# Order and spacing of the weight sums that a decoder step makes in DRAM

## The chip, the cores and the metric

One core of a Trainium2 chip runs the whole step as one program. The metric is the time of one execution in microseconds on the device. Three runs of the kernel before gave 1013.59, 1014.58 and 1017.05 us, median 1014.58. One more execution was taken with the hardware profiler: 1010.48 us, of which the span from the first to the last instruction is 1008.7 us.

Engines are named as in the profile: PE (TensorE, matmuls), PEld (its weight loads), DVE (VectorE), ACT (ScalarE), POOL (GpSimd), SP (SyncE, which issues most DMAs).

## The reference, cut to what matters

One layer of a hybrid decoder is applied to 512 prompt tokens and 8 x 4 sample tokens, 544 tokens in all, in float32:

```python
z = x @ w_in                                        # 1024 -> 6656: values and gates of two mixers
ca = silu(layer_norm(causal_dwconv(a_val * sigmoid(a_gate))))     # 31 taps
y_a = ca @ w_proj_a
hs = rg_lru(causal_dwconv(b_x))                     # 4 taps, two gate products, a scan
y_b = (hs * gelu(b_gate)) @ w_proj_b
mix = (sigmoid(g_a) * y_a + sigmoid(g_b) * y_b) @ w_out
x1 = layer_norm(ALPHA * x + mix)
ff = square(relu(x1 @ w_ff1)) @ w_ff2               # 1024 -> 4096 -> 1024
ple = sigmoid(x1 @ w_ple_gate) * (p @ w_ple_proj)
y = layer_norm(ALPHA * x1 + ff + ple)
```

The new convolution and scan states are outputs too. The change concerns w_ff1 and w_ff2 alone, and the time before they are used.

## The kernel before, in words

Activations lie with channels on the 128 partitions and the 544 tokens along the free dimension. Each float32 factor is split into a high part and the remainder (hi, lo), and a product is three matmuls: hi by hi, hi by lo, lo by hi. Weights are loaded by SP in chunks of 512 KB into `raw` (three buffers, line 38), ACT copies `hi`, DVE subtracts to get `lo`.

The step runs in the order of `ORDER` (line 52): input products of the two mixers (a, x, g, b, c), the gate products of the recurrence (r), then proj_b (p), the per-layer input (s) and proj_a (q), then w_out with the first layer norm, w_ple_gate, and last the MLP. While PE does the input products, DVE runs the 31-tap convolution (`ca`, line 734) as a chain of 30 multiply-adds for each of eight channel tiles. GpSimd makes the products of the sample tokens' taps (`prod`), the short convolution of the sample tokens (`cbs`, line 844), the running sum `sum_a`, the product of the input gate (`gg`), and after each scan the copy `hl` and the product `gate` (line 900).

The MLP uses a scheme of seven products in place of eight for blocks of two by two. A panel is one pair of output tiles; its weight has four blocks A11, A12, A21, A22. Of the seven products three use blocks as they are (A11, A22, A12) and four use sums of blocks:

- S3 = A11 + A21
- S1 = A21 + A22
- S2 = A22 + S3
- S4 = A12 + S2

No compute engine makes these sums. For each, SP copies one block from DRAM to a tile in DRAM (`sum...`), and then GpSimd issues a DMA that adds the other operand to that tile (line 246). S2 therefore needs a finished S3, and S4 a finished S2; S1 needs neither. There are 15 panels of w_ff1 (1 to 15, each sum 256 KB) and 4 of w_ff2, whose sums are made in two column parts c = 0 and 1 (each 384 KB): 60 + 32 = 92 sums, so 92 copies and 92 adds, 28.3 MB each.

The order of all instructions on all engines is written by a planner that runs when the program is built. `Clocks` (line 88) keeps a time for each engine and prices each operation; `Clocks.op` (line 125) lets a step start when its engine and its operands are ready by those clocks. An add is priced with 1.0 us of GpSimd and is ready some 3 us after its share of a common sum stream; a copy with 0.47 us of SP. `fill` (line 413) lets each engine take its next step as long as its clock is less than a given lead ahead of PE's. It asks `stream` (line 336) first, and `stream` asks `sum_stream` (line 261) first of all: with k = (PE's planner time - SUM_FROM) / SUM_EVERY, the n-th copy (from 0) may go when n < k + COPY_AHEAD, and the n-th add when n < k and its copy is out. So sums go out at an even pace, ahead of whatever else SP or GpSimd could do, and take their place on the two queues among the weight loads and among GpSimd's arithmetic. Each engine then works through its own list in order.

In the MLP, units (one block or sum of one panel) go through `fraw` on SP, `fhi` on ACT and `flo` on DVE (`add_unit`, line 1242); SP may be 7 units ahead of PE, ACT 5, DVE 4 (line 29). A unit that is a sum is loaded only once its add was issued (line 1280 issues it on the spot otherwise). The panels run in the order of line 34: w_ff1's panel 0 by plain products, then panels 1 to 3, then four passes over w_ff2 with further panels of w_ff1 after each: 4 to 6, 7 to 9, 10 to 13, and 14 and 15. Passes 0 and 1 over w_ff2 use part c = 0 of its sums, passes 2 and 3 part c = 1.

Of the kernel before, what the change touches and what calls it, by code (L numbers as in the profile page):

```python
# [9 lines left out]
F32 = mybir.dt.float32  # L10
F32R = mybir.dt.float32r
AF = mybir.ActivationFunctionType
OP = mybir.AluOpType
AX = mybir.AxisListType

P = 128
# [17 lines left out]
PANELS = [(1, p, None) for p in (1, 2, 3)]  # L34
for _g, _ps in enumerate(((4, 5, 6), (7, 8, 9), (10, 11, 12, 13), (14, 15))):
    PANELS += [(2, _p, _g) for _p in range(4)] + [(1, _p, None) for _p in _ps]
SUM_FROM, SUM_EVERY, COPY_AHEAD = 40.0, 6.0, 3
RAW_BUFS = 3
SPLIT_BUFS = 4
LOAD_AHEAD = 5  # L40
# [47 lines left out]
class Clocks:  # L88

    STEP = 0.13  # L90
    SETS = {AF.Sigmoid: 1, AF.Exp: 2, AF.Tanh: 2, AF.Sqrt: 3, AF.Gelu_apprx_tanh: 4}
# [68 lines left out]
def tile_hybrid_step(ctx: ExitStack, tc: tile.TileContext, I, O):  # L160
# [5 lines left out]
    dpool = ctx.enter_context(tc.tile_pool(name="sums", bufs=1, space=bass.MemoryType.DRAM))  # L166
# [22 lines left out]
    def cols(t, h):  # L189
# [4 lines left out]
    TE, V, S, G, DMA = (Engine(clocks, k, e) for k, e in  # L194
                        zip("TVSGD", (nc.tensor, nc.vector, nc.scalar, nc.gpsimd, nc.sync)))
# [37 lines left out]

    lead = [LEAD]
    sums, summed_up, to_copy, to_add = {}, set(), deque(), deque()
    for kind, n in [(1, p) for p in (1, 2, 3)] + [(2, p) for p in range(4)] + [(1, p) for p in range(4, 16)]:
        w = I["w_ff1" if kind == 1 else "w_ff2"][n]
        ncol = 512 if kind == 1 else 6 * P
        for c in range(kind):
            cs = slice(c * ncol, c * ncol + ncol)  # L240
            s = {nm: dpool.tile([P, ncol], F32, name=f"sum{kind}_{n}_{c}_{nm}") for nm in ("S3", "S1", "S2", "S4")}
            for nm, own, src in (("S3", w[0, :, cs], w[2, :, cs]), ("S1", w[2, :, cs], w[3, :, cs]),
                                 ("S2", w[3, :, cs], s["S3"]), ("S4", w[1, :, cs], s["S2"])):
                sums[kind, n, c, nm] = s[nm]
                to_copy.append(lambda to=s[nm], own=own: DMA.dma_start(to, own))
                to_add.append((lambda to=s[nm], src=src: G.dma_start(to, src, accum_op=OP.add, max_dma_last_dim=1024),
                               (kind, n, c, nm)))
    n_adds = len(to_add)

# [1058 lines left out]
    for n, k in in_turn():  # L1308
        kind, p, g = PANELS[n]
        if k == 1:  # L1310
            first_unit[kind, p if kind == 1 else g] = min(len(units), first_unit.get((kind, p if kind == 1 else g), INF))
        nm = FORM[k]
        q0, nq = (0, 4) if kind == 1 else GROUPS[g]
        key = (kind, p, 0 if kind == 1 else g // 2, nm)
        if nm in BLOCK:
            w, made = I["w_ff1" if kind == 1 else "w_ff2"][p, BLOCK[nm], :, q0 * P:(q0 + nq) * P], lambda: True
        else:
            c0 = 0 if kind == 1 else g % 2 * 3 * P
            w, made = sums[key][:, c0:c0 + nq * P], lambda key=key: key in summed_up
# [301 lines left out]
    for n, k in in_turn():  # L1621
        kind, p, g = PANELS[n]
# [96 lines left out]
```

## Time and profile before

| what | before |
|---|---|
| median of 3 runs | 1014.58 us |
| the profiled execution | 1010.48 us |
| its span | 1008.7 us |
| PE busy | 935.5 us |
| DVE busy | 793.7 us |
| ACT busy | 496.1 us |
| POOL busy | 254.2 us |
| first and last issue of a copy of the sums | 23.3 and 597.0 us |
| first and last issue of an add | 40.2 and 617.4 us |
| first and last load of a finished sum | 596.5 and 926.4 us |

Busy shares are means over stages with different bounds, so the table of stretches in the prediction is the better guide. In the rows of a timeline the columns are the start, the length, the engine and line, the operation with its output and inputs, the number of like instructions merged, and in brackets how long the engine had been idle before and what released it. Line 155 is the helper through which every instruction goes, so tiles and not lines tell the instructions apart. In the lists of waits, a row gives who waited for whom, the total in us, the number of times and the longest.

### The profile page before, as it was taken

Reading aid. Unit: us, or ns where it says so; the run is one execution under the profiler, and the core shown is the slowest. Engines: PE = TensorE matmul, PEld = TensorE weight load, DVE = VectorE, ACT = ScalarE, POOL = GpSimd, SP = SyncE. Lnnn points to the kernel's source line nnn. Section 1 sums busy time; section 2 is a strip of 40 time slices with the busy share of each in tenths; the row PEclk is TensorE's granted clock in tenths of the full one; section 3 lists DMA queues with packets and bytes.
Section 4 is the critical chain, followed back from the end, with each engine's and each line's share of the span. In section 5 each row is a group of like instructions: output and inputs, shape, how many; then the busy total and the mean of one; then the engine's idle time right before and its main releaser. Section 6 shows DMA issues by size and latency. Waiting matters only on the chain.

```text
span 1008.7 us, 18589 instructions
## 1 busy us (share of the span) xinstructions
PE 935.5 (93%) x7236; PEld 924.7 (92%) x7236; DVE 793.7 (79%) x1337; ACT 496.1 (49%) x875; POOL 254.2 (25%) x265
## 2 busy tenths in 40 slices
PE   8999798975989797999999999999999999999895
PEld 8999798975979797999999999989999899989895
DVE  5799999899997998793356883979688686777547
ACT  6422236623449622562233772775674655854601
POOL 0453755675637621210421211000000000000002
PEclk9999988997989899999999999999999999999998
DMA  8557689875889594967869784446546446446412
GB/s 298 147 152 185 180 200 262 196 175 138 183 214 202 136 212 130 229 160 196 260 155 253 173 225 54 149 133 188 174 138 204 148 146 218 147 144 204 133 48 84
DMA packets 125272, 175.81 MB, mean 174 GB/s; under 512 B 9920, under 2 KB 97344, under 8 KB 124224
## 3 DMA queue, kind: packets, MB, share of 16 engines
q1 hardware_dynamic: 96064, 146.31, 45.0%
q0 software_dynamic: 29120, 28.32, 20.3%
q8 instruction: 57, 0.93, 0.4%
q14 instruction: 31, 0.25, 0.1%
HBM read 167.57 MB, written 60.44 MB: 226 GB/s over the span
## 4 chain that ended last, share of the span: by engine, by line
PE 47%; DVE 29%; DMA 7%; ACT 7%; issue 5%; POOL 4%; SPq 0%; DVEq 0%; POOLq 0%; ACTq 0%
PE psq L155 13%; PE ps L155 13%; DVE ca L155 11%; PE f L155 8%; PE g L155 6%; DVE lo L155 4%; ACT fy L155 2%; ACT fhi L155 1%; DMA fraw<-sum_S 1%; DMA sum_S<-in_w_ff_dram 1%; DVE flo L155 1%; PE pps L155 1%; DVE th L155 1%; ACT fz L155 1%; DMA sum_S<-sum_S 1%
## 5 line engine op out<-in xcount | busy, mean ns | idle before, releaser
L155 DVE SCALAR_TENSOR_TENSOR ca<-u,par_a,ca 128x482 f32<-128x482 f32 (+29 forms) x240 | 176.3, 792 | 0.3
L155 ACT ACTIVATE hi<-raw 128x1024 fp32r<-128x1024 f32 (+3 forms) x109 | 99.9, 929 | 130.3 <-PE ps L155 52.6
L155 ACT ACTIVATE fhi<-fraw 128x512 fp32r<-128x512 f32 (+1 forms) x229 | 124.3, 571 | 60.5 <-DMA fraw<-sum_S 21.7
L155 DVE TENSOR_TENSOR flo<-fraw,fhi 128x512 fp32r<-128x512 f32 (+1 forms) x229 | 138.2, 620 | 17.7 <-ACT fhi L155 17.4
L155 DVE TENSOR_TENSOR lo<-raw,hi 128x1024 fp32r<-128x1024 f32 (+3 forms) x105 | 122.2, 1178 | 25.4 <-ACT hi L155 25.4
L155 POOL TENSOR_TENSOR y<-y,rows_g 128x512 f32<-128x512 f32 x2 | 3.1, 1550 | 379.1 <-ACT y L155 379.1
L155 POOL DMA_DIRECT2D sum_S<-sum_S x46 | 45.3, 985 | 171.5 <-DMA sum_S<-sum_S 91.2
L155 PE MATMUL f<-x1h,fhi 128*128 128x272 f32 x212 | 59.6, 294 | 5.1 <-DVE fz L155 3.5
L155 POOL DMA_DIRECT2D sum_S<-in_w_ff_dram x46 | 51.8, 1198 | 28.5 <-DMA sum_S<-in_w_ff_dram 27.1
L155 PE MATMUL f<-x1h,flo 128*128 128x272 f32 x212 | 58.6, 289 | 0.2 <-DVE flo L155 0.2
L155 PE MATMUL f<-x1l,fhi 128*128 128x272 f32 x212 | 58.4, 288 | 0.0
L155 PE MATMUL ps<-x0h,hi 128*128 128x288 f32 x104 | 23.9, 313 | 29.6 <-ACT gate L155 14.6
L155 PEld LDWEIGHTS ps<-x0h,hi 128*128 128x128 f32 x104 | 16.9, 200 | 31.5 <-ACT gate L155 15.5
L155 PEld LDWEIGHTS f<-x1h,fhi 128*128 128x128 f32 x212 | 39.0, 189 | 7.3 <-DVE fz L155 5.4
L155 DVE TENSOR_TENSOR acc<-acc,g 128x272 f32<-128x272 f32 x80 | 34.8, 434 | 12.9 <-PE g L155 12.1
L155 PEld LDWEIGHTS f<-x1h,flo 128*128 128x128 f32 x212 | 38.9, 188 | 0.5 <-DVE flo L155 0.5
L155 PEld LDWEIGHTS f<-x1l,fhi 128*128 128x128 f32 x212 | 39.0, 189 | 0.0
L155 PE MATMUL psq<-x1l,hi 128*128 128x288 f32 (+1 forms) x128 | 36.9, 288 | 0.0
L155 PE MATMUL psq<-x1h,lo 128*128 128x288 f32 (+1 forms) x128 | 36.8, 288 | 0.0
L155 PE MATMUL psq<-x1h,hi 128*128 128x288 f32 (+1 forms) x128 | 36.8, 288 | 0.0
L155 POOL TENSOR_TENSOR prod<-ctx_a,par_a 128x248 f32<-128x248 f32 x32 | 30.9, 1150 | 0.0
L155 ACT ACT_TABLE_LOAD x20 | 25.7, 1283 | 1.1 <-PEq L1709 0.7
(1994 smaller groups left out, 3385.9 us busy)
## 6 DMA issues: line engine op xcount, KB each, us to landing
raw<-in_w_in_dram SPq DMA_DIRECT2D x51, 512.0 KB, 5.0
fraw<-in_w_ff_dram SPq DMA_DIRECT2D x65, 256.0 KB, 3.5
sum_S<-in_w_ff_dram SPq DMA_DIRECT2D x60, 256.0 KB, 5.3
fraw<-sum_S SPq DMA_DIRECT2D x60, 256.0 KB, 3.3
sum_S<-in_w_ff_dram SPq DMA_DIRECT2D x32, 384.0 KB, 5.8
fraw<-sum_S SPq DMA_DIRECT2D x64, 192.0 KB, 2.9
fraw<-in_w_ff_dram SPq DMA_DIRECT2D x48, 192.0 KB, 3.1
sum_S<-in_w_ff_dram POOLq DMA_DIRECT2D x30, 256.0 KB, 5.4
```

Source lines behind the costliest of these rows:

```text
L155: return fn(out, *args, **kw)
```

## The change

The sums are made in another order, at another pace, and copies run further ahead.

- Order: before, panel by panel, and within a panel S3, S1, S2, S4 in a row. After, in seven sets of three or four panels, and within a set form by form: S3 of all its panels, then S1 of all, S2 of all, S4 of all. The sets are w_ff1 1 to 3; w_ff2 part c = 0; w_ff1 4 to 6; 7 to 9; w_ff2 part c = 1; w_ff1 10 to 12; 13 to 15. Before, both parts of w_ff2 came right after w_ff1's panels 1 to 3.
- Distance: S4 comes three or four issues after the S2 that it needs (one before), S2 six or eight after its S3 (two before).
- Pace: SUM_FROM from 40.0 to 25.0, SUM_EVERY from 6.0 to 7.2, COPY_AHEAD from 3 to 4.

The sums themselves, their number and their sizes stay.

```diff
-SUM_FROM, SUM_EVERY, COPY_AHEAD = 40.0, 6.0, 3
+SUM_FROM, SUM_EVERY, COPY_AHEAD = 25.0, 7.2, 4
...
-    for kind, n in [(1, p) for p in (1, 2, 3)] + [(2, p) for p in range(4)] + [(1, p) for p in range(4, 16)]:
-        w = I["w_ff1" if kind == 1 else "w_ff2"][n]
-        ncol = 512 if kind == 1 else 6 * P
-        for c in range(kind):
-            cs = slice(c * ncol, c * ncol + ncol)
-            s = {nm: dpool.tile([P, ncol], F32, name=f"sum{kind}_{n}_{c}_{nm}") for nm in ("S3", "S1", "S2", "S4")}
-            for nm, own, src in (("S3", w[0, :, cs], w[2, :, cs]), ("S1", w[2, :, cs], w[3, :, cs]),
-                                 ("S2", w[3, :, cs], s["S3"]), ("S4", w[1, :, cs], s["S2"])):
-                sums[kind, n, c, nm] = s[nm]
-                to_copy.append(lambda to=s[nm], own=own: DMA.dma_start(to, own))
-                to_add.append((lambda to=s[nm], src=src: G.dma_start(to, src, accum_op=OP.add, max_dma_last_dim=1024),
+    SETS = ([(1, p, 0) for p in (1, 2, 3)], [(2, p, 0) for p in range(4)], [(1, p, 0) for p in (4, 5, 6)],
+            [(1, p, 0) for p in (7, 8, 9)], [(2, p, 1) for p in range(4)], [(1, p, 0) for p in (10, 11, 12)],
+            [(1, p, 0) for p in (13, 14, 15)])
+    for ps_ in SETS:
+        for nm in ("S3", "S1", "S2", "S4"):
+            for kind, n, c in ps_:
+                w = I["w_ff1" if kind == 1 else "w_ff2"][n]
+                ncol = 512 if kind == 1 else 6 * P
+                cs = slice(c * ncol, c * ncol + ncol)
+                s = sums[kind, n, c, nm] = dpool.tile([P, ncol], F32, name=f"sum{kind}_{n}_{c}_{nm}")
+                own, src = {"S3": (0, w[2, :, cs]), "S1": (2, w[3, :, cs]), "S2": (3, sums.get((kind, n, c, "S3"))),
+                            "S4": (1, sums.get((kind, n, c, "S2")))}[nm]
+                to_copy.append(lambda to=s, own=w[own, :, cs]: DMA.dma_start(to, own))
+                to_add.append((lambda to=s, src=src: G.dma_start(to, src, accum_op=OP.add, max_dma_last_dim=1024),
                                (kind, n, c, nm)))
```

## The prediction

> **What bounds the kernel now.** I read the page's busy shares first, then the waits, the table of stretches, and last the timelines of GpSimd and VectorE where the change acts.
>
> ```profile
> PE 935.5 (93%) x7236; PEld 924.7 (92%) x7236; DVE 793.7 (79%) x1337; ACT 496.1 (49%) x875; POOL 254.2 (25%) x265
> q1 hardware_dynamic: 96064, 146.31, 45.0%
> q0 software_dynamic: 29120, 28.32, 20.3%
> ```
> TensorE is busy 93% of 1008.7 us. q0 is GpSimd's DMA queue, which carries nothing but the 92 adds. The stretches say more than the mean; their columns are the stretch, its length, busy us of PE, PEld, DVE, ACT and POOL, granted clock, DMA share, GB/s:
>
> ```profile
> 100.00:400.00 300.00, 256.87 (x1927) 253.97 (x1925) 282.12 (x369) 136.85 (x187) 166.85 (x161) 0.92 0.80 186
> 400.00:600.00 200.00, 199.11 (x1553) 198.24 (x1554) 134.55 (x234) 95.98 (x169) 43.38 (x45) 0.99 0.80 203
> 617.00:711.00 94.00, 90.01 (x707) 88.28 (x706) 76.01 (x159) 58.17 (x124) 0.88 (x1) 1.00 0.48 142
> 617.00:946.00 329.00, 314.61 (x2465) 309.48 (x2463) 249.50 (x516) 203.00 (x431) 0.88 (x1) 1.00 0.51 158
> ```
> Between 100 and 400 us VectorE is the bound: 17.9 of 300 us idle, while TensorE idles 43 and runs at a clock of 0.92. From 400 on TensorE is the bound: 0.9 us idle in 200, and 14.4 in the 329 of the MLP.
>
> The change is aimed at this:
>
> ```profile
> POOL sum_S L155 <- DMA sum_S<-in_w_ff_dram: 107.4, 22, 11.7
> POOL sum_S L155 <- DMA sum_S<-sum_S: 91.2, 16, 9.9
> ```
> GpSimd stands 198.6 us in 38 waits in front of an add, for the DMA that makes its source or its own tile. That is a fifth of the span, on an engine that is busy a quarter of it. So the question is not how long it waits but what stands behind it on its queue.
>
> **What the removed waits are worth.** Two waits of the same length, from the timelines of GpSimd and VectorE (start, length, instruction, idle before it and its releaser):
>
> ```profile
> 148.38 0.94 POOL L155 DMA_DIRECT2D sum_S<-sum_S  x1 [9.19 <-DMA sum_S<-sum_S]
> 151.24 0.64 POOL L155 COPY st_u<-u 128x30 f32<-128x30 f32 x1 [0.65 <-DVE u L155]
> ...
> 194.15 1.52 POOL L155 DMA_DIRECT2D sum_S<-sum_S  x1
> 204.91 0.94 POOL L155 DMA_DIRECT2D sum_S<-sum_S  x1 [9.24 <-DMA sum_S<-sum_S]
> 205.52 2.05 POOL L155 COPY hl<-th 128x9 f32<-128x9 f32 x1
> ```
> ```profile
> 203.10 1.28 DVE L155 TENSOR_TENSOR_SCAN th<-aa,gg 128x544 f32<-128x544 f32 x1
> ```
> After the first, the next arithmetic on GpSimd still waits 0.65 us for VectorE: the wait cost nothing. The second is the one place I found where it cost something: the scan ends at 204.38, the copy that needs it starts at 205.52, so 1.1 us are lost, and they go on through the gate product to a wait of VectorE (hb0l, below). Behind the other waits of over 4 us I find, in the same timeline, the next non-DMA instruction released later by VectorE or ScalarE. So of 198.6 us of waits 1.1 us reach the bound. The chain of waits seems to say more, since it names sum DMAs. But there a step is put down to a semaphore that fell by chance:
>
> ```profile
> 132.13 4.07 DMA sum_S<-in_w_ff_dram
> 136.20 0.36 POOL cb L155
> ```
> ```profile
> 134.76 0.63 POOL L155 TENSOR_TENSOR cbs<-ctx_b,par_r 128x64 f32<-128x64 f32 x1
> 135.47 0.62 POOL L155 TENSOR_TENSOR cbs<-cbs,cbs 128x64 f32<-128x64 f32 x1
> 136.19 0.70 POOL L155 TENSOR_SCALAR cb<-cbs,par_r 128x32 f32<-128x32 f32 x2
> ```
> GpSimd was at work without a gap until cb, and waited for no DMA. If my reading misses others, the cap is what VectorE idles at all:
>
> ```profile
> 119.97 4.34 DVE L155 TENSOR_TENSOR cb2l<-cb,cb2h 128x544 fp32r<-128x544 f32 x1 [2.14 <-ACT cb2h L155]
> 137.28 0.73 DVE L155 TENSOR_TENSOR cb4l<-cb,cb4h 128x544 fp32r<-128x544 f32 x1 [1.37 <-ACT cb4h L155]
> 193.77 0.72 DVE L155 TENSOR_TENSOR cb6l<-cb,cb6h 128x544 fp32r<-128x544 f32 x1 [2.53 <-ACT cb6h L155]
> 209.62 0.73 DVE L155 TENSOR_TENSOR hb0l<-gate,hb0h 128x544 fp32r<-128x544 f32 x1 [2.08 <-ACT hb0h L155]
> 306.68 2.50 DVE L155 TENSOR_TENSOR lo<-raw,hi 128x1024 fp32r<-128x1024 f32 x1 [1.11 <-ACT hi L155]
> 312.14 0.67 DVE L155 TENSOR_REDUCE conv_s<-prod 128x16 f32<-128x496 f32 x1 [2.96 <-POOL prod L155]
> 313.84 0.67 DVE L155 TENSOR_REDUCE conv_s<-prod 128x16 f32<-128x496 f32 x1 [1.03 <-POOL prod L155]
> ```
> These seven are 13.2 of the 17.9 us. The cb rows follow GpSimd's short convolution, which has no add inside. The last two follow the products, and there adds do stand in front:
>
> ```profile
> 304.43 0.97 POOL L155 DMA_DIRECT2D sum_S<-sum_S  x1
> 305.08 1.61 POOL L155 DMA_DIRECT2D sum_S<-in_w_ff_dram  x1
> 305.86 4.54 POOL L155 TENSOR_TENSOR sum_a<-sum_a,ca 128x544 f32<-128x544 f32 x2
> ```
> Two adds hold GpSimd from 304.43 to 305.86, 1.4 us. Issues get 7.2/6.0 = 1.2 times rarer, so about one add in six is gone here, and with the chance that neither falls there I take 0.7 us, between 0 and 1.4.
>
> **When the adds run.** Add k is due at planner time 40 + 6.0 k before and 25 + 7.2 k after; the two meet at k = 12.5, planner time 115. The trace ties planner to chip:
>
> ```profile
> 40.21 1.95 POOL L155 DMA_DIRECT2D sum_S<-in_w_ff_dram  x2
> ...
> 617.35 0.88 POOL L155 DMA_DIRECT2D sum_S<-sum_S  x1 [3.65 <-DMA sum_S<-sum_S]
> ```
> ```profile
> 651.95 1.50 PE f2d L155 x12
> ```
> Add 0 (due 40) starts at 40.2 and add 91 (due 586) at 617.4, after its wait. In the MLP twelve matmuls take 1.50 us, 0.125 each, which is the planner's own price (0.0118 + 272/2400), so there the planner runs one to one. After the change add 91 is due at 680.2, so about 94 us later, near 711. By then 78 adds are out at planner time 586; 14 adds and, four issues ahead, 10 copies move into the stretch 617 to 711, all 256 KB panels of w_ff1. The panels that need the last ones (13 to 15) come late in the MLP, so no load waits for a sum.
>
> DMA prices: q0's 20.3% of 1008.7 us over 28.32 MB is 7.2 us of all 16 engines per MB, so 1.9 us for an add of 256 KB and 2.8 for one of 384; q1's 45.0% over 146.31 MB is 3.1 us per MB, so 0.8 us for a copy of 256 KB. Into 617 to 711 come 14 x 1.9 + 10 x 0.8 = 35 us, and its DMA share goes from 0.48 to about 0.85, near the 0.80 of 100 to 400. There the weight loads meet them:
>
> ```profile
> fraw<-sum_S SPq DMA_DIRECT2D x60, 256.0 KB, 3.3
> ACT fhi L155 <- DMA fraw<-sum_S: 21.7, 16, 3.7
> ACT fhi L155 <- DMA fraw<-in_w_ff_dram: 18.0, 14, 3.2
> PE g L155 <- ACT fhi L155: 1.6, 1, 1.6
> PE f L155 <- ACT fhi L155: 1.0, 1, 1.0
> ```
> A load lands 3.3 us after its issue. ScalarE waited 39.7 us for such loads over the whole MLP, and only 2.6 us of that reached TensorE, one part in fifteen, because splits run up to five units of 1.5 us ahead. If each of some 58 loads in the stretch lands 1 us later and ScalarE waits all of it, TensorE loses 58/15 = 3.9 us; if the lead hides it, nothing. The nearest row, the 1 in 15, with a third of the loads late, gives 1.3; I take 1. The upper end: TensorE's 4.0 us of idle in this stretch trebles, +8. The ten copies also stand on SP's queue between loads, at the 0.51 us of this row, 5 us in all; that is in the same bounds:
>
> ```profile
> L155 SPq DMA_DIRECT2D sum_S<-in_w_ff_dram x92: 490/512/1570, 23.3 to 597.0; - x92
> ```
>  GpSimd's queue is empty of arithmetic there until the last rows of the output, so its waits delay no one.
>
> Between 100 and 400 the DMA load falls. Before, sums 12 to 43 are all of 384 KB; after, only 12 to 27 are, then 24 sums of 256 KB. In planner time 115 to 346 that is 14.3 MB of adds before (31 large, 8 small by the due times) against 10.3 after (15 and 17), and copies alike: 4.0 x (7.2 + 3.1) = 41 us of DMA time less in some 270. I price it at nothing: of VectorE's idle there only the 1.11 us row hangs on a loaded tile. Its bounds are -1.3 and 0; what it saves TensorE stays hidden as long as VectorE sets the end of the stretch. At the start the first copies go out some 18 us of planner time earlier, into the first loads; four copies of 0.8 us are at most 3 us of DMA time and I take 0.
>
> **The sum.** -1.1 - 0.7 + 1.0 = -0.8 us on the profiled execution: 1010.5 becomes 1009.7 (1.8 us of it lie around the span). The median of the runs before is 1014.58, 4.1 above that execution, so 1013.8. What this kernel's runs can tell from no change is about 0.3%, 3 us.
>
> **Rivals.** *Faster: the stretch to 400 us shortens.* The planner puts each step in order by its clocks, and GpSimd's clock loses the wait of S4 for S2; its steps are then placed otherwise, and steps of VectorE behind them. For it: all but the ACT hi row of the idle above comes by way of GpSimd, 12.1 us, and this row:
>
> ```profile
> L155 DVE TENSOR_TENSOR t<-aa,par_r x10: 141/166/5270, 201.0 to 340.5; 128x8 f32<-128x8 f32 x10
> ```
> An operation of 0.17 us takes 5.27 when it falls beside GpSimd's arithmetic, so one collision more or less is 5.1 us. Price: a third to all of 12.1, -4 to -12, so 1002.6 to 1010.6. Against it: the adds themselves lie beside none of those rows but two. In the Trainium skill, SBUF — State Buffer, section Who interferes with whom, the two engines hold a shared read path exclusively, and a VectorE instruction with two SBUF inputs stands against a GpSimd one that reads SBUF; the trace agrees with its 5.27 us. By that rule the collisions move with any new order, to either side.
>
> *Slower: the MLP's loads lose to the sums.* Place: 617 to 711; mechanism: fhi late on ScalarE, whose evacuations queue behind it, then TensorE. It decides once loads land later by more than the lead covers: a wait of 3.7 us on ScalarE, the longest, came with at most 1.6 on TensorE, so by 2 us and more on several loads in a row. Price +3 to +8: 1017.6 to 1022.6. For it: a share of 0.85. Against: the 1 part in 15. In the Trainium skill, DMA: Bandwidth & Descriptors, section Issuing engines are not separate DMA queues, transfers of all issuing engines run on the same 16 engines and interleave; by that rule moving sums here takes time from loads, which speaks against the change. No row of this trace has 14 adds beside these loads.
>
> *Slower by order:* one collision more in the stretch to 400: +5.1, 1018.9.
>
> *No effect:* the adds go on waiting for copies that SP issues late; nothing stands behind those waits, so 1014.6.
>
> **How the numbers follow.** My forecast of nearly no change has 0.33 and no effect 0.05: 0.38 within 0.3%. Faster by over 0.3% has 0.37, since 12 us of idle hang on GpSimd and a new order may free a third. Slower has 0.25: 0.17 for the loads, 0.08 for a collision. The likeliest case's own range is 1011.5 to 1016.6. For 8 in 10 I go down to 1005.0, 9 of the 12 us, and up to 1021.0, leaving out a tenth on each side.
>
> **What would show it.** GpSimd's waits on sum DMAs fall from 198.6 to under 50 us. VectorE's idle between 100 and 400 stays between 12 and 18 us, and the scan-to-copy gap at the first gate closes. Adds run to about 711; DMA share of 617 to 711 is about 0.85; TensorE's idle there is 4 to 7 us. I am wrong if VectorE ends its convolutions more than 4 us away from 398, or if TensorE idles over 10 us between 617 and 711.

## The result and the profile after

The changed kernel took 1023.77 us (median of 4 runs, 1023.21 to 1024.42) against 1014.09 for the kernel before beside it: a ratio of 1.0091, 95% interval 1.0068 to 1.0113. It is slower by about 9 us. The forecast was 1013.8, nearly no change. The profiled execution of after took 1023.32 us, that of before 1010.48, which is below all its other runs; so the traces differ by 12.8 us, 3 more than the medians. From the page of after, its first and third parts:

```profile
PE 943.1 (92%) x7236; PEld 932.0 (91%) x7236; DVE 791.3 (77%) x1337; ACT 497.2 (49%) x875; POOL 245.7 (24%) x265
...
q1 hardware_dynamic: 96064, 146.31, 44.8%
q0 software_dynamic: 29120, 28.32, 19.6%
```

The engines run as many instructions as before and the queues move the same bytes. Of the 12.8 us TensorE idles 5.2; for the other 7.6 it is busy longer with the same 7236 matmuls. The question is in which stage this costs time. Three matmuls that every run has mark the stages; the view of a tile gives their first start: `lnamu`, the first matmul of the layer norm behind the convolutions, `ln1mu`, the first of the layer norm behind w_out, and `f`, whose first and last fall on the MLP. Before, and then after (columns: instruction, count, shortest, median and longest ns, first to last start):

```profile
L155 PE MATMUL lnamu<-lnash,ones x2: 415/512/608, 400.3 to 401.2; 128*128 128x288 f32 x1, 128*128 128x256 f32 x1
L155 PE MATMUL ln1mu<-ln1sh,ones x2: 282/289/296, 550.9 to 578.0; 128*128 128x288 f32 x1, 128*128 128x256 f32 x1
L155 PE MATMUL f<-x1h,fhi x212: 283/289/397, 627.7 to 942.6; 128*128 128x272 f32 x106
```
```profile
L155 PE MATMUL lnamu<-lnash,ones x2: 415/511/607, 406.4 to 407.3; 128*128 128x288 f32 x1, 128*128 128x256 f32 x1
L155 PE MATMUL ln1mu<-ln1sh,ones x2: 282/288/294, 562.5 to 589.6; 128*128 128x288 f32 x1, 128*128 128x256 f32 x1
L155 PE MATMUL f<-x1h,fhi x212: 283/288/428, 639.3 to 955.6; 128*128 128x272 f32 x106
```

From these rows come three stretches, used for every run below: A, from the start to `lnamu`; B, from `lnamu` to `ln1mu`, which holds proj_b, proj_a and w_out; D, from the first to the last `f`. The change costs 6.1 us in A (400.3 to 406.4), 5.5 in B (150.6 to 156.1) and 1.4 in D (314.9 to 316.3).

**Stretch B.** The view of stretches over B, before, after, and for e2_order, a kernel of the experiments below (stretch, length, busy us of PE, PEld, DVE, ACT, POOL, clock, DMA share, GB/s):

```profile
400.30:550.90 150.60, 149.98 (x1161) 149.12 (x1161) 91.32 (x140) 60.30 (x91) 33.39 (x33) 0.98 0.80 206
406.40:562.50 156.10, 151.55 (x1161) 150.44 (x1162) 91.61 (x140) 60.48 (x91) 33.42 (x29) 0.97 0.86 214
402.20:552.80 150.60, 149.33 (x1160) 148.44 (x1161) 91.64 (x140) 60.39 (x91) 36.65 (x33) 0.99 0.95 236
```

TensorE, which idled 0.6 us in B, idles 4.5, and is busy 1.6 us longer with the same matmuls. The mean DMA share is no measure of the loss: it is 0.86 after, and 0.95 in e2_order, which loses nothing here. The place is in the timelines of the engines between 534 and 552 us, here after:

```profile
534.30 0.42 POOL L155 COPY sum<-res 128x288 f32<-128x288 f32 x1 [12.17 <-DVE res L155]
534.74 3.87 POOL L155 DMA_DIRECT2D sum_S<-sum_S  x4
...
537.66 0.37 SPq L155 DMA_DIRECT2D raw<-in_w_out_dram  x1
...
548.76 1.15 ACT L155 ACTIVATE hi<-raw 128x512 fp32r<-128x512 f32 x2 [8.56 <-DMA raw<-in_w_out_dram]
...
549.42 1.29 DVE L155 TENSOR_TENSOR lo<-raw,hi 128x512 fp32r<-128x512 f32 x2 [7.56 <-ACT hi L155]
550.63 0.45 DVE L155 SCALAR_TENSOR_TENSOR res<-xr,psq 128x288 f32<-128x288 f32 x1
...
551.22 0.58 PE L155 MATMUL psq<-mix0h,hi 128*128 128x288 f32 x1 [3.08 <-DVE res L155]
```

Read it downwards. GpSimd waits 12.17 us for VectorE; four adds have come due meanwhile and stand behind it on its queue. With nothing to wait for, all four go out within 3.9 us. Each is 384 KB, 2.8 us of all 16 DMA engines by the prediction's price, so 11 us of DMA work. SP's load for w_out is issued 2.9 us later and is usable at 548.76, 11.1 us after its issue. ScalarE waits for it, VectorE for ScalarE, and VectorE's evacuations `res` stand behind that `lo` on its queue, so the tile `psq` that TensorE is to write next comes free late: 3.08 us of idle, and 0.92 more at 557. The 1.6 us follow at once: from 551 to 555 us, behind the wait, the granted clock is 0.52 and then 0.62, and in e5_late_add, behind a wait of 3.15 us at the same place, 0.50 for 6 us. Where this wait is missing (before, e6, e7) the clock at this place is 1.00. The DMA view of 525 to 560 us shows the same from the transfers' side (issues, KB each, median us to landing):

```profile
sum_S<-sum_S POOLq DMA_DIRECT2D x4, 384.0 KB, 13.2
...
raw<-in_w_ple_proj_dram SPq DMA_DIRECT2D x1, 512.0 KB, 12.7
```

The same place in the kernel before:

```profile
528.43 0.42 POOL L155 COPY sum<-res 128x288 f32<-128x288 f32 x1 [12.34 <-DVE res L155]
528.90 0.88 POOL L155 DMA_DIRECT2D sum_S<-sum_S  x1
529.46 2.14 POOL L155 DMA_DIRECT2D sum_S<-in_w_ff_dram  x2
537.64 0.88 POOL L155 DMA_DIRECT2D sum_S<-sum_S  x1 [6.04 <-DMA sum_S<-in_w_ff_dram]
544.81 0.88 POOL L155 DMA_DIRECT2D sum_S<-sum_S  x1 [6.29 <-DMA sum_S<-sum_S]
...
531.78 0.38 SPq L155 DMA_DIRECT2D raw<-in_w_out_dram  x1
...
539.80 1.16 ACT L155 ACTIVATE hi<-raw 128x512 fp32r<-128x512 f32 x2 [5.15 <-DMA raw<-in_w_out_dram]
```

GpSimd stood just as long behind the same copy, and three adds left at once behind it. But then S2 had to wait 6.04 us for its S3 and S4 6.29 us for its S2, so five adds went out over 16 us; they were of 256 KB, too. The load was usable 8.0 us after its issue (531.78 to 539.80) against 11.1, ScalarE waited 5.15 us for it, and TensorE not at all. On this reading the waits that the change removes had been a brake; the experiments test it.

**Stretch A.** The first part of the loss lies in the first 50 us, in the timelines of GpSimd and VectorE after, and then before:

```profile
34.81 0.86 POOL L155 DMA_DIRECT2D sum_S<-in_w_ff_dram  x1
35.41 7.01 POOL L155 TENSOR_TENSOR prod<-ctx_a,par_a 128x248 f32<-128x248 f32 x8
...
35.19 7.26 DVE L155 TENSOR_TENSOR z<-e,d 128x10 f32<-128x10 f32 x1
42.48 0.17 DVE L155 TENSOR_TENSOR z<-z 128x10 f32<-128x10 f32 x1
...
48.30 0.52 PE L155 MATMUL ps<-x0h,lo 128*128 128x288 f32 x2 [2.66 <-DVE lo L155]
```
```profile
33.47 6.80 POOL L155 TENSOR_TENSOR prod<-ctx_a,par_a 128x248 f32<-128x248 f32 x8
...
33.82 0.57 DVE L155 TENSOR_TENSOR z<-e,d 128x10 f32<-128x10 f32 x1
34.42 0.85 DVE L155 TENSOR_TENSOR z<-z 128x10 f32<-128x10 f32 x1
35.30 0.81 DVE L155 TENSOR_SCALAR s<-z 128x10 f32<-128x10 f32 x1
```

Before, GpSimd's eight products begin ahead of VectorE's chain on ten elements, and the chain gets on at some 0.8 us a step. After, an add stands in front of the products (the stream begins at 25 us), they begin 0.22 us behind the first step of the chain, and that one step takes 7.26 us, as long as all eight products. VectorE's time from this step of the chain to its next split: 33.82 to 43.37 before, 35.19 to 47.02 after, 9.55 us against 11.83, so 2.3 us lost, and TensorE waits 2.66 us for the split. This is no accident of one run: all five traced kernels with the add at this place (after, e1, e4, e6, e8) have this step at 7.26 to 7.28 us, and none of the seven without it. For VectorE between 100 and 400 us after, the view of stretches has 20.4 us of idle:

```profile
100.00:400.00 300.00, 263.64 (x1968) 261.01 (x1967) 279.62 (x371) 137.68 (x187) 148.41 (x155) 0.93 0.65 161
```

### The profile page after: what moved, and what is told of

It reads as the page before. It is cut to its first block, busy times and chain, and to the rows that moved or that the text cites. A ratio compares the mean times of both kernels' runs of the same rounds, so it can differ in the third digit from the quotient of the medians.

```text
span 1021.5 us, 18612 instructions
## 1 busy us (share of the span) xinstructions
PE 943.1 (92%) x7236; PEld 932.0 (91%) x7236; DVE 791.3 (77%) x1337; ACT 497.2 (49%) x875; POOL 245.7 (24%) x265
## 4 chain that ended last, share of the span: by engine, by line
PE 53%; DVE 22%; ACT 9%; DMA 7%; POOL 4%; issue 4%; SPq 1%; DVEq 0%; ACTq 0%; POOLq 0%
PE ps L155 20%; PE psq L155 12%; PE f L155 8%; DVE ca L155 8%; PE g L155 6%; DVE lo L155 3%; DMA raw<-in_w_in_dram 2%; ACT fhi L155 1%; ACT fy L155 1%; DMA raw<-in_w_ple_gate_dram 1%; PE pps L155 1%; ACT fz L155 1%; ACT hi L155 1%; DVE th L155 1%; POOL cbs L155 1%
## 5 line engine op out<-in xcount | busy, mean ns | idle before, releaser
L155 DVE SCALAR_TENSOR_TENSOR ca<-u,par_a,ca 128x508 f32<-128x508 f32 (+28 forms) x240 | 177.1, 795 | 0.4
L155 DVE TENSOR_TENSOR lo<-raw,hi 128x1024 fp32r<-128x1024 f32 (+3 forms) x105 | 119.9, 1156 | 40.6 <-ACT hi L155 40.6
L155 POOL DMA_DIRECT2D sum_S<-in_w_ff_dram x46 | 49.5, 1277 | 132.2 <-DMA sum_S<-in_w_ff_dram 127.9
L155 POOL DMA_DIRECT2D sum_S<-sum_S x46 | 43.0, 1148 | 79.3 <-DMA sum_S<-in_w_ff_dram 70.7
L155 POOL TENSOR_TENSOR prod<-ctx_a,par_a 128x248 f32<-128x248 f32 x32 | 34.0, 1190 | 0.0
L155 PE MATMUL ps<-x0h,lo 128*128 128x288 f32 x104 | 22.8, 303 | 6.2 <-DVE lo L155 6.2
```

What stands on the lines that cost most here:

```text
L155: return fn(out, *args, **kw)
```

## The experiments

Three theories stood at the beginning. *Brake*: the removed waits had spaced the adds. *Plan*: the new constants put instructions of VectorE, ScalarE and GpSimd in another order (TensorE's is the same). *Large sums*: the sums of 384 KB now lie in the w_out stage. Ratios are to the kernel before, run beside them; stretches are of the profiled runs, one each, and they spread. A: e6_brake_w_out is the same program as after up to add 52, at the end of A, and has 402.9 in its shortest run where after has 406.4. D lies between 314.9 and 319.5 in all but e1 and e10, in good part by the granted clock: taken in steps of 20 us, it is 0.91 in no step of before, in one of after, e6 and e9, and in three of e4, e5 and e7, and a step at 0.91 loses 1.8 us. The profiled run of e1 was the longest of its runs, those of e2 and e6 were the shortest. The kernels e3, e4, e6 and e7 make other sums than the MLP needs, so only their times are of use.

| run | ratio, 95% interval | A | B | D |
|---|---|---|---|---|
| before | 1 | 400.3 | 150.6 | 314.9 |
| after | 1.0091, 1.0068 to 1.0113 | 406.4 | 156.1 | 316.3 |
| e1_pace | 1.0069, 1.0047 to 1.0091 | 411.4 | 150.5 | 321.5 |
| e2_order | 1.0011, 0.9993 to 1.0029 | 402.2 | 150.6 | 317.2 |
| e3_no_wait | 1.0001, 0.9983 to 1.0019 | 404.1 | 151.7 | 316.1 |
| e4_brake | 1.0024, 1.0008 to 1.0040 | 405.0 | 149.9 | 318.6 |
| e5_late_add | 1.0058, 1.0036 to 1.0080 | 402.3 | 155.8 | 319.4 |
| e6_brake_w_out | 1.0019, 1.0002 to 1.0037 | 402.9 | 150.8 | 315.9 |
| e7_both | 0.9983, 0.9962 to 1.0003 | 402.4 | 149.6 | 318.0 |
| e8_swap | 1.0056, 1.0033 to 1.0079 | 407.6 | 151.5 | 319.5 |
| e9_mended | 1.0000, 0.9986 to 1.0014 | 403.1 | 150.2 | 317.4 |
| e10_last | 1.0065, 1.0042 to 1.0087 | 402.3 | 151.7 | 325.0 |

**The halves of the change.** e1_pace is the kernel before with the new constants, e2_order the changed kernel with the old ones:

```diff
-SUM_FROM, SUM_EVERY, COPY_AHEAD = 40.0, 6.0, 3
+SUM_FROM, SUM_EVERY, COPY_AHEAD = 25.0, 7.2, 4
```

> The old order of sums (panel by panel) with the new pace (25.0, 7.2, copies 4 ahead). Its lists on PE, DVE and ACT are those of the changed kernel; only which sum each copy and add makes differs. Theory 1 (the waits of S2 for S3 and of S4 for S2 were a brake: without them three or four adds go out back to back and hold the 16 DMA engines while weight loads wait): 1012 to 1017 us, since the brake is there. Theory 2 (the new pace moved 42 lines of VectorE's list and 19 of ScalarE's, to a worse plan): 1020 to 1024 us, all of the loss. Theory 3 (the large sums of w_ff2, part 1, now fall into the w_out stage): 1013 to 1018 us, since here they are made early.

> The new order of sums with the old pace (40.0, 6.0, copies 3 ahead). Its lists on PE, DVE and ACT are those of the kernel before. Theory 1 (brake): 1019 to 1027 us, GpSimd's waits on sum DMAs fall and adds come in groups of three or four. Theory 2 (plan): 1013 to 1015 us. Theory 3 (large sums in the w_out stage): 1013 to 1016 us, since at this pace they are due between 352 and 442 us of planner time, ahead of that stage.

The order alone costs nothing that can be measured, 1.0011, and moves no arithmetic of the engines. The pace alone costs 1.0069. It has the lists of after, the brake of before, and a B of 150.5: so the 5.5 us of B need order and pace together, and A has a cost of the pace's own. (As its profiled run was its longest, its A of 411.4 overstates that.)

**The brake, taken away and put back.** In e3_no_wait, the kernel before with S2 adding A11 and S4 adding A21 in place of S3 and S2, nothing waits for an earlier sum; in e4_brake, the changed kernel, the third add of each four waits for the first and the fourth for the third. The planner's clocks are told the old operands.

```diff
-                                 ("S2", w[3, :, cs], s["S3"]), ("S4", w[1, :, cs], s["S2"])):
+                                         ("S2", w[3, :, cs], s["S3"], w[0, :, cs]),
+                                         ("S4", w[1, :, cs], s["S2"], w[2, :, cs])):
...
+                    nc.gpsimd.dma_start(to, other, accum_op=OP.add, max_dma_last_dim=1024)
```
```diff
+                back = {2: 2, 3: 1}.get(k % 4)
+                other = made[k - back] if back and made[k - back].shape == s.shape else None
...
+                    nc.gpsimd.dma_start(to, src if other is None else other, accum_op=OP.add, max_dma_last_dim=1024)
```

> The kernel before, lists of all engines unchanged, but S2 adds block A11 in place of the finished S3 and S4 adds A21 in place of the finished S2: the same bytes from DRAM, no wait of an add for another add. The sums, and so the MLP, come out other than the reference's. Theory 1 (brake): 1018 to 1026 us. Theories 2 and 3: 1013 to 1015 us, for neither plan nor place of a sum changes. What I predicted from (the waits cost about 1 us and give nothing): 1013 us.

> The changed kernel, lists of all engines unchanged, but of each four adds in issue order the third adds the tile that the first made and the fourth the tile that the third made (same sizes): the pattern of waits of the kernel before on the new plan and pace. The sums, and so the MLP, come out other than the reference's. Theory 1 (brake): 1013 to 1018 us. Theory 2 (plan): 1022 to 1025 us. Theory 3 (large sums in the w_out stage): 1019 to 1024 us, the first layer norm's stage still 5 us late.

On the old plan taking the waits away costs nothing (1.0001): there 256 KB sums lie in the w_out stage, and B is 151.7. But the test is weaker than it looks, since at the place of the loss the fourth and fifth add of e3 still wait 3.05 and 9.50 us, now for their own copies, which run only three ahead. On the new plan the brake takes the ratio from 1.0091 to 1.0024, and B is back at 149.9 although the large sums are still there. Large sums alone are thus not the cause. That a missing brake alone is not either is shown by e10 below, where four sums of 256 KB leave together: it takes both.

**The two places by themselves.** e5_late_add issues the second add with the third, behind GpSimd's products; e6_brake_w_out has the brake of e4 on adds 52 to 67 alone; e7_both has both edits.

```diff
+                k = len(to_add)
...
+                    held_back.append((to, src))
+                    if k != 1:
+                        for t, x in held_back:
+                            nc.gpsimd.dma_start(t, x, accum_op=OP.add, max_dma_last_dim=1024)
+                        held_back.clear()
```
```diff
+                back = {2: 2, 3: 1}.get(k % 4) if 52 <= k < 68 else None
```

> The changed kernel, with the second add issued right behind GpSimd's eight products prod (with the third add) instead of right ahead of them; every list of PE, DVE and ACT stays as it was. Port theory: that add moved GpSimd's products by 0.5 us against VectorE's chain of small operations on z, so that one operation on 10 elements took 7.26 us; with the add behind them the chain runs in steps of about 0.8 us as before, VectorE reaches its next split 2.3 us earlier, TensorE's idle of 2.7 us at 48 us is under 0.8, and the ratio to before falls from 1.0091 to about 1.007. Rival (the early copies and adds delay the weight loads of the first 50 us): the idle of 2.7 us at 48 us stays, since copies and adds still move the same bytes, and so does the ratio.

> The changed kernel, with the wait of every third and fourth add on the one ahead of it put back for adds 52 to 67 alone, the sums of w_ff2's second part that fall into the w_out stage. For that the S2 and S4 issues among these add a tile made one or two issues earlier instead of their own operand, so that part of the MLP's sums is not the reference's. Lists of PE, DVE and ACT stay. Burst theory: TensorE's idle of 3.1 and 0.9 us in that stage goes, the stretch from the first statistics of the attention mixer to the first of the first layer norm falls from 156.1 to 150 to 151 us, and the ratio from 1.0091 to about 1.0036. Rival (the wait was needed everywhere, from 100 us on): the stretch falls by less than 2 us, and the ratio stays above 1.007, since the full brake gave 1.0024.

> Both edits at once: the second add behind the products, and the wait put back for adds 52 to 67 (again with another operand for some S2 and S4 there, so that part of the MLP's sums is not the reference's). If the two costs are separate and add up, 2.3 and 5.5 us of the 9.2 go and the ratio is about 1.0014, 0.5 to 1 us under the kernel with the full brake and without the late add. If what is left is the plan's own late weight loads between 140 and 310 us, it stays above 1.002.

The ratio of e5 is 1.0058, lower by 0.0033 (3.4 us, expected 2.3; the intervals overlap). The same edit on top of e6, in e7, takes off 0.0036. The timelines of e5 show the step as expected:

```profile
33.98 6.77 POOL L155 TENSOR_TENSOR prod<-ctx_a,par_a 128x248 f32<-128x248 f32 x8
40.70 2.63 POOL L257 DMA_DIRECT2D sum_S<-in_w_ff_dram  x3
...
43.75 2.35 DVE L155 TENSOR_TENSOR lo<-raw,hi 128x1024 fp32r<-128x1024 f32 x2
```

No small operation of VectorE takes over 2 us there, its split begins at 43.75, and TensorE has no idle of 1 us or more near 48. The bytes of the early copies and adds are the same, so the rival of late loads fails at this place.

e6 comes to 1.0019, as good as the brake on all 92 adds; the 7.3 us that it takes off are more than the 5.5 of B, with wide intervals. Its B, from the view of the tiles, is 553.7 - 402.9 = 150.8:

```profile
L155 PE MATMUL lnamu<-lnash,ones x2: 415/512/609, 402.9 to 403.8; 128*128 128x288 f32 x1, 128*128 128x256 f32 x1
L155 PE MATMUL ln1mu<-ln1sh,ones x2: 282/288/294, 553.7 to 580.9; 128*128 128x288 f32 x1, 128*128 128x256 f32 x1
```

So a brake on sixteen adds out of 92 is enough. Three of these adds still leave together, at 541.66, but only after the first, at 532.01, has landed, and the load of w_out issued between them is usable after 7.8 us. e7 gives 0.9983: the two edits take 0.0108 off, and singly 0.0033 and 0.0072. They add up, and nothing of the loss is left.

**Where else the large sums could go.** e8_swap makes the sums of w_ff2's second part third instead of fifth, at planner time 111 to 341; e10_last makes them last, beside the MLP (with the late add of e5). Both stay form by form. e9_mended leaves them in their place and makes that one set panel by panel again, with the late add.

```diff
-    SETS = ([(1, p, 0) for p in (1, 2, 3)], [(2, p, 0) for p in range(4)], [(1, p, 0) for p in (4, 5, 6)],
-            [(1, p, 0) for p in (7, 8, 9)], [(2, p, 1) for p in range(4)], [(1, p, 0) for p in (10, 11, 12)],
+    SETS = ([(1, p, 0) for p in (1, 2, 3)], [(2, p, 0) for p in range(4)], [(2, p, 1) for p in range(4)], [(1, p, 0) for p in (4, 5, 6)],
+            [(1, p, 0) for p in (7, 8, 9)], [(1, p, 0) for p in (10, 11, 12)],
```
```diff
-            [(1, p, 0) for p in (7, 8, 9)], [(2, p, 1) for p in range(4)], [(1, p, 0) for p in (10, 11, 12)],
-            [(1, p, 0) for p in (13, 14, 15)])
+            [(1, p, 0) for p in (7, 8, 9)], [(1, p, 0) for p in (10, 11, 12)],
+            [(1, p, 0) for p in (13, 14, 15)], [(2, p, 1) for p in range(4)])
```
```diff
+        for nm, (kind, n, c) in ([(nm, p) for p in ps_ for nm in forms_] if ps_[0][2] else
+                                 [(nm, p) for nm in forms_ for p in ps_]):
```

> The changed kernel with the set of w_ff2's second part moved from fifth to third place, so that the sums of 384 KB run at planner time 111 to 341 and the w_out stage gets sums of 256 KB, still three in a row and without a brake. Lists of PE, DVE and ACT are the changed kernel's. If bursts hurt by their bytes (four of 384 KB hold the DMA engines 11 us, three of 256 KB 5.6), the w_out stretch falls from 156.1 to 150 to 152 us, and the stretch to 400 us grows by 0 to 5 as the large sums meet the weight loads there: ratio 1.004 to 1.009. If the number of adds in a row counts and not their size, the w_out stretch stays at 155 or more and the ratio at 1.009 or above.

> All sums as the reference needs them: the changed kernel with the second add behind GpSimd's products, and the set of w_ff2's second part alone made panel by panel again (S3, S1, S2, S4 of one panel in a row), so that in the w_out stage S4 waits for the S2 right ahead of it. Lists of PE, DVE and ACT stay. If the two costs found are the whole of the loss, this is e7_both with the real operands: the w_out stretch is 150 to 151 us, the stretch to 400 us is within 2 us of before's, and the ratio to before is about 0.998, between 0.995 and 1.002. If the tile that an add reads matters (in e7_both some adds read a tile written just before, with no own operand to fetch), the w_out stretch stays over 153 us and the ratio above 1.003.

> All sums as the reference needs them: the changed kernel with the second add behind GpSimd's products, and the set of w_ff2's second part moved to the end, to planner time 572 to 680, most of it beside the MLP; still form by form. Lists of PE, DVE and ACT stay. Burst theory: the w_out stretch has bursts of 256 KB and falls to 150 to 152 us; the MLP's loads run up to seven units ahead, so bursts of 384 KB there cost TensorE 0 to 4 us; ratio 0.998 to 1.003. Rival (the MLP's loads lose to the sums, as one of the rivals of the prediction had it): the MLP grows by 5 us and more, and the ratio stays at 1.005 or above.

In e8, B falls to 151.5 with sums of 256 KB. That does not yet tell bytes from number: in sets of three, S4 waits for an S2 only three issues back, and so three adds leave at 536.27 and the fourth 3.57 us behind them, after a wait. e10 has the answer at the same place, with four adds of 256 KB in a row:

```profile
531.05 1.79 POOL L257 DMA_DIRECT2D sum_S<-sum_S  x2
532.17 2.49 POOL L257 DMA_DIRECT2D sum_S<-in_w_ff_dram  x2
```

They are as many as in after and go out as fast, but the next w_out load is usable after 9.0 us, TensorE waits 1.01 us where after waits 3.08, and B is 151.7: it is the bytes of a burst that count. At the same time A grows in e8 from after's 406.4 to 407.6, although the run began 1.5 us ahead of after's at the first products (28.65 against 30.14 us). The place is VectorE's splits near 306 us; e8 first, and then after:

```profile
308.28 2.34 POOL L155 TENSOR_TENSOR sum_a<-sum_a,ca 128x544 f32<-128x544 f32 x1
310.30 6.83 POOL L155 TENSOR_TENSOR prod<-ctx_a,par_a 128x248 f32<-128x248 f32 x8
...
305.91 13.45 DVE L155 TENSOR_TENSOR lo<-raw,hi 128x1024 fp32r<-128x1024 f32 x3
```
```profile
309.40 1.06 ACT L155 ACTIVATE hi<-raw 128x1024 fp32r<-128x1024 f32 x1 [10.57 <-DMA raw<-in_w_in_dram]
...
309.87 3.50 DVE L155 TENSOR_TENSOR lo<-raw,hi 128x1024 fp32r<-128x1024 f32 x2
...
312.25 8.76 POOL L155 TENSOR_TENSOR prod<-ctx_a,par_a 128x248 f32<-128x248 f32 x8
```

In e8 three splits fall beside GpSimd's `sum_a` and all eight `prod` and take 13.45 us. After, two are done 1.1 us into the products and take 3.50, and it is GpSimd's products that take longer, 8.76 us against 6.83. The profile of e1, which has the large sums there too, is like that of e8 (13.54 us for three splits at 310.22). So the collision is seen in both kernels that have large sums there on the new plan; by which load or wait they bring it about was not isolated.

In e10 the MLP pays instead of B. Its first 100 us, from the table of stretches, before, after, and e10:

```profile
627.70:727.70 100.00, 97.00 (x756) 95.29 (x756) 82.34 (x170) 66.41 (x141) 0.00 (x0) 1.00 0.53 161
```
```profile
639.30:739.30 100.00, 95.65 (x741) 93.57 (x742) 81.03 (x167) 65.08 (x137) 9.67 (x11) 1.00 0.82 217
```
```profile
630.90:730.90 100.00, 91.39 (x681) 89.03 (x682) 77.36 (x160) 59.99 (x127) 11.30 (x11) 0.97 0.91 231
```

TensorE idles 3.0, 4.4 and 8.6 us at DMA shares of 0.53, 0.82 and 0.91. The clock of 0.97 is a part of it. D grows to 325.0, 5.6 us over that of e5, which has the same late add and its large sums in the w_out stage; 5.4 of that is idle time of TensorE in D (12.5 and 17.9 us). So my burst theory's 0 to 4 us was too small and the rival was right here.

e9 gives 1.0000: the loss of 9 us is gone with two small edits. GpSimd's adds in the w_out stage are apart again:

```profile
531.64 0.99 POOL L258 DMA_DIRECT2D sum_S<-sum_S  x1
540.97 0.95 POOL L258 DMA_DIRECT2D sum_S<-sum_S  x1 [8.34 <-DMA sum_S<-sum_S]
541.58 2.87 POOL L258 DMA_DIRECT2D sum_S<-in_w_ff_dram  x2
```

As e7 and e9 have the lists of after, *Plan* is no cause of the loss by itself. e9 is no gain over the kernel before. In its profiled run one step of the chain on ten elements took 5.88 us, with the add behind the products. Of the four traced kernels with the late add it is the only one with a step over 2 us, so the late add does not exclude the slow step.

## Why the prediction was wrong

- **The waits.** "So of 198.6 us of waits 1.1 us reach the bound" is the step that failed. I asked only what stands behind a waiting GpSimd, and found next to nothing, which e2 and e3 bear out: on the old plan these waits cost nothing. The term of -1.1 even came at its place: the scan at the first gate ends at 216.54 and the copy behind it starts at 216.61. But I did not ask what the waits keep apart. The next resource behind an add is the 16 DMA engines, and there the wait set the distance between transfers. Its loss, together with sums of 384 KB at this place, costs 5.5 us in B, for which the sum -1.1 - 0.7 + 1.0 has no term; e4, e6 and e9 get them back.
- **The stage that I left out.** I priced the DMA load of 100 to 400 us, where it falls, and of the MLP, where it rises. For 400 to 600 I had a row with a DMA share of 0.80 and 0.9 us of idle, the least slack of all, and worked out nothing, though the new order and pace put sums of 384 KB in place of 256 there.
- **The even pace.** My arithmetic took adds to go out 7.2 us apart. They are due so, but on the chip four stood behind one copy that waited 12.17 us.
- **GpSimd's waits falling under 50 us.** Wrong: they moved from sums to copies.

```profile
POOL sum_S L155 <- DMA sum_S<-in_w_ff_dram: 198.6, 25, 30.0
POOL sum_S L155 <- DMA sum_S<-sum_S: 8.5, 3, 4.6
```

  It is 207.1 us in 28 waits. The longest, 30.0 us, holds up nobody, since GpSimd has nothing else to do in the MLP.
- **The start.** "Four copies of 0.8 us are at most 3 us of DMA time and I take 0" looked at the copies. What cost 2.3 us is the add that then stood in front of GpSimd's products. The rival "one collision more" had the mechanism, at 5.1 us and a chance of 0.08, but named no place for it. In the Trainium skill, SBUF — State Buffer, section Who interferes with whom, the two engines hold a shared read path exclusively; the 7.26 us beside products of 7.01 agree.
- **VectorE's idle of 12 to 18 us, convolutions within 4 us of 398.** Idle was 20.4, and `lnamu` came 6.1 us later. Of that, 2.3 are the collision, and 1.4 were there at 30 us already (the first product `u` at 30.14 against 28.77); the runs have this first product anywhere from 28.65 to 31.92, without order by kernel, so I count it as spread. The rest, 2.4, I cannot put to one instruction; it is no more than the spread of A, for e6, the same program up to there with the same collision, has 402.9. Nor is it VectorE's longest wait in that stretch, 5.78 us at 201.03: e7 has 5.14 at the same instruction, neither of the two costs, and an A of 402.4.
- **Why the plan moved.** I argued that a lost wait in GpSimd's clock would reorder other engines. The order alone moves no arithmetic (e2); the three constants do.
- **The MLP.** Right for the first 100 us of D: a share of 0.85 forecast and 0.82 measured, TensorE's idle 4.4 us where I had 4 to 7 (before, in the same 100 us, 3.0). The last add was issued at 724.8 and not near 711, as the MLP began 11.6 us later. But this idle did not last: over all of D TensorE idles 12.5 us, and 13.0 before. D's 1.4 us more are busy time, at a granted clock of 0.83 in the ten us from 819.3, long after the last add. That they are close to my 1.0 is luck. In the Trainium skill, DMA: Bandwidth & Descriptors, section Issuing engines are not separate DMA queues, transfers of all issuers run on the same 16 engines and interleave. The trace agrees, but most clearly in the w_out stage, where a load issued behind four adds took 11.1 us and 8.0 before. I weighed this rule against the wrong stage.

## What to carry to other kernels

Before a wait is removed because nobody queues behind it, ask what it keeps apart: the adds here cost nothing while some waited for the one before them, and 5.5 us once four of 384 KB could leave together. A pace written into a planner holds only where the issuing engine is free; here, behind one that waited, everything that had come due left as one burst. Such a burst is to be priced by its bytes against the next load's lead, not by the mean DMA share, which was higher in a kernel that lost nothing. Look first at the stage with the least slack, even if the change was not made for it.

## What the runs showed of the hardware

- One operation on ten elements took 7.26 us beside eight products of GpSimd that began 0.22 us later; when the products began 0.35 us earlier, the same chain went on at about 0.8 us a step. An add on GpSimd's queue in front of the products, which start 0.6 us behind it, decided which: a step of 7.26 to 7.28 us came in all five traces with it and in none of the seven without, where the longest was 5.88.
- Four adds of 384 KB issued within 3.9 us landed after a median of 13.2 us, and a 512 KB load issued 4.1 us after the first of them after 12.7.
- Behind a wait of TensorE of 3.08 us the granted clock was 0.52 and then 0.62 for 4 us, behind one of 3.15 us 0.50 for 6 us; over the ten us with the wait of 1.01 us in e10 it was 1.00.
